# Five rows of one chunk, dealt unevenly over the DMA engines: Pool's software queue over 5 and 11 of them, sync over four

## The chip, the cores and the metric

The kernel runs on one core of a Trainium2 chip. The metric is the device time of one execution in microseconds. A profile's span is shorter than the time by about 1.3 us. "Before" and "changed" are the two kernels; the chunks are counted from 0 in the code, so that "the fourth chunk" is chunk 3.

The profile counts 16 DMA engines. A DMA shows there as packets: a 4 MB chunk as 128 packets of 32 KB. Its semaphore gets sixteen increments, which are read here as the ends of the sixteen engines' shares; in the kernel before, those of chunk 1's load lie between 22.30 and 22.77 us.

## The reference, cut to what matters

```python
x = randn(16, 2048, 256)          # float32: 32768 rows of 1 KB
y = x @ W + scale * (((x @ lora_A) * lora_E) @ lora_B)
```

The kernel folds the low-rank part into one 256x256 matrix (`weff`). What remains is to read 33.55 MB of `x`, multiply, and write 33.55 MB.

## The kernel before

`x` is cut into 8 chunks of 4 MB. In a chunk, partition p holds 32 consecutive rows, so that a chunk's load is one DMA of 128 partitions with 32 KB each. Six chunks have a home in SBUF; the result overwrites the chunk and is stored from there.

```python
x_chunks = x_flat.rearrange("(c p b) k -> c p b k", p=P, b=ROWS)     # P = 128, ROWS = 32
...
ORDER = ["L0", "L1", "L2", "L3", "L4", "L5",
         "S0", "S1", "L6", "L7", "S2", "S3", "S4", "S5", "S6", "S7"]
...
def load(pc):                                   # in sync_program
    c, s, e = pc
    if c == N_HOMES - 1:
        sync.wait_ge(s_weff, 1)
    if c >= N_HOMES:
        sync.wait_ge(stored_of[c - N_HOMES], 16)
    ins = sync.dma_start(out=home(c)[:, s:e, :], in_=x_chunks[c, :, s:e, :])
    return ins.then_inc(loaded[pc], 16)
...
for g in range(N_GROUPS):                       # in gpsimd_program; a group is 4 rows
    ...                                         # waits for the piece of x that starts here
    gpsimd.tensor_copy(out=stage[g % NS][:], in_=home(c)[:, b:b + CG, :]).then_inc(s_stage, 1)
```

Pool casts to bf16, PE transposes, ACT copies, PE multiplies, DVE copies the result back over the chunk.

Of the kernel before, what the change touches and what calls it, by code (L numbers as in the profile page):

```python
# [13 lines left out]
ROWS = 32  # L14
# [9 lines left out]
EARLY_AFTER = 1  # L24

HELD = N_HOMES - 1

CG = 4
GPC = ROWS // CG
# [8 lines left out]
def kernel(  # L38
# [13 lines left out]
    N, K = x_flat.shape  # L52
# [5 lines left out]
    x_chunks = x_flat.rearrange("(c p b) k -> c p b k", p=P, b=ROWS)  # L58
    y_chunks = out_flat.rearrange("(c p b) m -> c p b m", p=P, b=ROWS)

    sbuf, psum, sem = nc.alloc_sbuf_tensor, nc.alloc_psum_tensor, tc.alloc_semaphore
# [21 lines left out]
    loaded = {pc: sem(f"loaded_{pc[0]}_{pc[1]}") for pc in pieces}  # L83
    set_up_loaded = {n: sem(f"loaded_{n}") for n in ("w", "a", "b", "e")}
    stored_of = {c: sem(f"stored_{c}") for c in range(N_CHUNKS - N_HOMES)}
    stored_rest = nc.alloc_semaphore("stored_rest")
    s_ident = sem("ident_made")
    s_pe_set_up = sem("pe_set_up")
    s_ate = sem("ate_made")
# [10 lines left out]
    def home(c):  # L100
        return homes[c % N_HOMES]

    sync, gpsimd, scalar, vector, tensor = nc.sync, nc.gpsimd, nc.scalar, nc.vector, nc.tensor
# [17 lines left out]

    nc.at_finalize(ahead_of_entry_barrier)

    def sync_program():
        def load(pc):
            c, s, e = pc
            if c == N_HOMES - 1:
                sync.wait_ge(s_weff, 1)
            if c >= N_HOMES:
                sync.wait_ge(stored_of[c - N_HOMES], 16)  # L130
            ins = sync.dma_start(out=home(c)[:, s:e, :], in_=x_chunks[c, :, s:e, :])
            return ins.then_inc(loaded[pc], 16)

        opening.append(load(pieces[0]).ins.name)
        for step in ORDER:
            c = int(step[1:])
            if step[0] == "L":
                for pc in pieces:
                    if pc[0] == c and pc != pieces[0]:
                        load(pc)  # L140
                if c == EARLY_AFTER:

                    sync.wait_ge(s_first, 1)
                    sync.dma_start(out=y_chunks[0, :16, 0, :32], in_=home(0)[:16, 0, :32]).then_inc(s_early, 16)
            else:
                sync.wait_ge(s_chunk, c + 1)
                if c == 0:
                    sync.wait_ge(s_early, 16)
                sync.dma_start(out=y_chunks[c], in_=home(c)[:]).then_inc(stored_of.get(c, stored_rest), 16)

    def gpsimd_program():
        gpsimd.memset(ident[:], 0.0).then_inc(s_ident, 1)  # L152
        gpsimd.wait_ge(s_ident, 1)
        gpsimd.affine_select(  # L154
            out=ident[:],
            in_=ident[:],
            compare_op=ALU.not_equal,
            fill=1.0,
            base=0,
            pattern=[[-1, P]],  # L160
            channel_multiplier=1,
        ).then_inc(s_ident, 1)
        for g in range(N_GROUPS):
            c, b = g // GPC, g % GPC * CG
            for pc in pieces:
                if pc[0] == c and pc[1] == b:
                    gpsimd.wait_ge(loaded[pc], 16)
            if (c, b) == (HELD, 0):
                for held_by in stored_of.values():
                    gpsimd.wait_ge(held_by, 16)  # L170
            if g >= NS:
                gpsimd.wait_ge(s_turned, g - NS + 1)
            gpsimd.tensor_copy(out=stage[g % NS][:], in_=home(c)[:, b:b + CG, :]).then_inc(s_stage, 1)  # L173

        gpsimd.wait_ge(s_turned, N_GROUPS - NS + 1)
        gpsimd.drain().then_inc(s_stage, 2)
# [91 lines left out]
    with tc.tile_critical(no_gpsimd_drain=True):  # L268
        sync_program()
        gpsimd_program()  # L270
        scalar_program()
        vector_program()
        tensor_program()
# [35 lines left out]
```

## Time and profile before

| | before |
|---|---|
| time, median (all runs of the first comparison) | 161.78 us (161.56 to 161.97) |
| span of the profiled run | 160.5 us |
| sync's DMA queue, share of 16 engines | 97.9% |
| busiest compute engine | PE, 59% |

From the profile's page of the kernel before. "DMA" is the busy share of the 16 DMA engines in 40 slices of the span, in tenths; "GB/s" is what they moved in each slice. The queue lines give packets, MB, and the share of 16 engines' span. The last lines are of the chain that ended last and of two groups of instructions (busy us, mean ns, idle us before them and what ended it).

```profile
span 160.5 us, 2160 instructions
...
DMA  7999999999999999999999999999999999999993
GB/s 262 432 425 466 449 393 425 490 392 408 498 400 392 492 400 400 400 417 466 425 400 451 457 392 433 474 402 425 466 400 433 466 408 433 449 425 417 441 449 155
...
q1 hardware_dynamic: 2624, 67.11, 97.9%
q10 hardware_dynamic: 352, 0.30, 0.5%
...
HBM read 33.85 MB, written 33.56 MB: 420 GB/s over the span
...
PE 11%; DVE 1%; issue 0%
PE psum_y L236 8%; PE psum_xt L228 4%; DVE home L213 1%
...
L173 POOL CAST stage<-home 128x1024 bf16<-128x1024 f32 x64 | 66.3, 1040 | 47.5 <-PE psum_xt L228 21.4
...
L208 DVE TENSOR_TENSOR weff<-home,psum_y 128x512 bf16<-128x512 f32 x1 | 0.7, 689 | 5.9 <-DMA home<-in_W_dram 5.9
```

The DMA engines are busy in every slice, while the chain of work that ended last covers only 12% of the span: after it, stores drain. `weff` waits for the load of W.

From the view of stretches of the same profile: stretch in us from the span's start, its length, busy us of PE, its weight loads, DVE, ACT and Pool with their instruction counts, then PE's granted clock, the DMA share, and GB/s.

```profile
core 0: us, PE busy (x) PEld busy (x) DVE busy (x) ACT busy (x) POOL busy (x), PEclk, DMA share, GB/s
4.00:24.00 20.00, 14.95 (x86) 11.41 (x87) 8.15 (x8) 8.00 (x8) 9.44 (x10) 1.00 1.03 436
24.00:40.00 16.00, 15.99 (x147) 14.92 (x148) 13.88 (x13) 12.05 (x12) 13.12 (x13) 1.00 0.99 426
40.00:46.00 6.00, 6.00 (x58) 5.58 (x57) 5.66 (x5) 4.51 (x6) 4.65 (x6) 1.00 1.02 437
46.00:58.00 12.00, 12.00 (x113) 11.16 (x111) 11.24 (x10) 9.32 (x10) 9.57 (x10) 1.00 1.02 438
```

The trace also records each DMA packet (start, duration, bytes) and each increment of a DMA's semaphore. A 32 KB packet takes 1.213 us, and the next on its engine starts 3 ns before it ends, hence 27.1 GB/s an engine. The first landings of chunks 1 to 4 are 9.7 us apart (22.30, 32.02, 41.73, 51.45 us), eight such packets: an engine moves 8 of a chunk's 128 partitions. The sixteen increments of the last store are read as the ends of the sixteen engines. This listing is worked out from those records, in us from the span's start:

```
last store, before:   158.45 158.47 158.48 158.70 158.75 158.78 158.80 158.83
                      158.88 158.89 158.90 158.93 159.18 159.44 159.62 160.42
chunk 1 loaded, before: 22.30 to 22.77        chunk 4 loaded, before: 51.45 to 51.92
```

One engine is 0.8 us behind the next. Its 32 KB packets took about 80 ns more than the others', from 100 to 124 us, while stores and compute ran together (two more did from 64 to 66 us). To relieve such an engine is the obvious idea.

### The profile page before, as it was taken

What the parts mean: (1) busy time and instruction counts of PE and PEld (TensorE: products, weight loads), DVE (VectorE), ACT (ScalarE), POOL (GpSimd) and SP (SyncE); (2) the same over time, 40 slices, a digit from 0 to 9 for tenths busy, and PEclk for the clock granted to TensorE, in tenths of its full rate; (3) what the DMA queues carried; (4) which work ended last, traced back from release to release, by engine and by line L of the source; (5) the groups of instructions that cost most, each with busy time, mean ns of one, the idle gap of its engine ahead of it and who ended that gap; (6) DMA issues with size and microseconds to landing.
All of it is one profiled execution on the core that took longest, in us unless ns stands there. A gap on an engine that the chain in (4) does not pass through costs nothing. (4 is left out here: it accounts for less than half of the span.)

```text
span 160.5 us, 2160 instructions
## 1 busy us (share of the span) xinstructions
PE 94.2 (59%) x782; PEld 83.9 (52%) x782; DVE 79.5 (50%) x66; ACT 66.0 (41%) x65; POOL 67.0 (42%) x70
## 2 busy tenths in 40 slices
PE   0585979999999999400019999999990000000000
PEld 0354869999999999300017999899990000000000
DVE  0102796999999999700003799899993000000000
ACT  3240667777777777400005577777740000000000
POOL 1542648777777777000045577777700000000000
PEclk9999999999999999955555999999998555555555
DMA  7999999999999999999999999999999999999993
GB/s 262 432 425 466 449 393 425 490 392 408 498 400 392 492 400 400 400 417 466 425 400 451 457 392 433 474 402 425 466 400 433 466 408 433 449 425 417 441 449 155
DMA packets 2979, 67.43 MB, mean 420 GB/s; under 512 B 528, under 2 KB 544, under 8 KB 672
## 3 DMA queue, kind: packets, MB, share of 16 engines
q1 hardware_dynamic: 2624, 67.11, 97.9%
q10 hardware_dynamic: 352, 0.30, 0.5%
q14 instruction: 3, 0.02, 0.0%
HBM read 33.85 MB, written 33.56 MB: 420 GB/s over the span
## 5 line engine op out<-in xcount | busy, mean ns | idle before, releaser
L213 DVE COPY home<-psum_y 128x1024 f32<-128x1024 f32 x64 | 78.3, 1225 | 30.0 <-PE psum_y L236 25.3
L173 POOL CAST stage<-home 128x1024 bf16<-128x1024 f32 x64 | 66.3, 1040 | 47.5 <-PE psum_xt L228 21.4
L193 ACT COPY xt<-psum_xt 128x1024 bf16<-128x1024 bf16 x64 | 64.7, 1012 | 49.8 <-PE psum_xt L228 49.8
L236 PE MATMUL psum_y<-weff,xt 128*128 128x256 bf16 x512 | 69.4, 281 | 2.6 <-PEq L221 2.5
L236 PEld LDWEIGHTS psum_y<-weff,xt 128*128 128x128 bf16 x512 | 51.4, 101 | 9.6 <-issue 3.2
L228 PE MATMUL psum_xt<-ident,stage 128*128 128x128 f32 x264 | 42.5, 287 | 18.6 <-PEq L221 18.6
L228 PEld LDWEIGHTS psum_xt<-ident,stage 128*128 128x128 f32 x264 | 33.1, 149 | 21.1 <-issue 20.2
L198 DVE TENSOR_SCALAR home<-psum_y,e_sb 16x256 f32<-16x256 f32 x1 | 0.5, 472 | 6.6 <-DMA e_sb<-in_lora_E_dram 6.6
L208 DVE TENSOR_TENSOR weff<-home,psum_y 128x512 bf16<-128x512 f32 x1 | 0.7, 689 | 5.9 <-DMA home<-in_W_dram 5.9
L248 PE MATMUL psum_y<-ident,home 128*16 128x128 f32 x2 | 0.6, 394 | 5.1 <-DMA home<-in_lora_A_dram 5.1
L248 PEld LDWEIGHTS psum_y<-ident,home 128*16 128x16 f32 x2 | 0.1, 87 | 5.1 <-issue 5.1
L193 ACT ACT_TABLE_LOAD x1 | 1.3, 1283 | 2.5 <-issue 2.5
L254 PE MATMUL psum_y<-home 16*128 16x256 f32 x4 | 2.1, 670 | 0.2 <-DMA home<-in_lora_B_dram 0.2
L254 PEld LDWEIGHTS psum_y<-home 16*128 16x128 f32 x4 | 1.2, 319 | 0.8 <-DMA home<-in_lora_B_dram 0.6
L152 POOL MEMSET ident<- 128x128 f32 x1 | 0.2, 204 | 0.7 <-SPq L268 0.7
L154 POOL TENSOR_SCALAR_AFFINE_SELECT ident<-ident 128x128 f32<-128x128 f32 x1 | 0.3, 292 | 0.2 <-POOL ident L152 0.2
L290 POOL MEMSET const-float32-0.0<- 128x1 f32 x1 | 0.1, 98 | 0.2 <-issue 0.2
L290 POOL MEMSET const-bfloat16-1.0<- 128x1 bf16 x1 | 0.1, 101 | 0.0
L290 POOL MEMSET const-uint8-127<- 128x1 uint8 x1 | 0.1, 101 | 0.0
L290 POOL MEMSET const-float32-1.0<- 128x1 f32 x1 | 0.1, 98 | 0.0
## 6 DMA issues: line engine op xcount, KB each, us to landing
out_dram<-home SPq DMA_DIRECT2D x8, 4096.0 KB, 39.7
home<-in_x_dram SPq DMA_DIRECT2D x7, 4096.0 KB, 20.8
home<-in_x_dram SPq DMA_DIRECT2D x2, 1024.0 KB, 5.7
home<-in_x_dram SPq DMA_DIRECT2D x1, 2048.0 KB, 11.5
home<-in_W_dram ACTq DMA_DIRECT2D x1, 256.0 KB, 10.9
home<-in_lora_A_dram ACTq DMA_DIRECT2D x1, 16.0 KB, 4.9
e_sb<-in_lora_E_dram ACTq DMA_DIRECT2D x1, 0.1 KB, 5.5
home<-in_lora_B_dram ACTq DMA_DIRECT2D x1, 16.0 KB, 5.8
```

Source lines behind the costliest of these rows:

```text
L152: gpsimd.memset(ident[:], 0.0).then_inc(s_ident, 1)
L154: gpsimd.affine_select(out=ident[:], in_=ident[:], compare_op=ALU.not_equal, fill=1.0, base=0, pattern=[[-1, P]], channel_multiplier=1,).t ...
L173: gpsimd.tensor_copy(out=stage[g % NS][:], in_=home(c)[:, b:b + CG, :]).then_inc(s_stage, 1)
L193: scalar.copy(out=xt[g % NX][:], in_=halves).then_inc(s_xt, 1)
L198: vector.tensor_scalar(out=ate, in0=psum_y[0][:R, :KT, :P], scalar1=e_sb[:], scalar2=float(scale), op0=ALU.mult, op1=ALU.mult,).then_inc(s ...
L208: vector.tensor_add(out=weff[:], in0=w_sb, in1=psum_y[1][:, :KT, :]).then_inc(s_free, NY)
L213: vector.tensor_copy(out=home(c)[:, b:b + CG, :], in_=psum_y[g % NY][:]).then_inc(s_free, 1)
L228: ins = tensor.transpose(psum_xt[i % NT][:, b, :], words[:, b, :], ident[:])
L236: ins = tensor.matmul(psum_y[i % NY][:, b, :], xt[i % NX][:, b, t, :], weff[:, t, :], start=(t == 0), stop=(t == KT - 1),)
L248: ins = tensor.transpose(psum_y[0][:R, t, :P], a_sb[:, t, :], ident[:])
L254: ins = tensor.matmul(psum_y[1][:, t, :], ate[:, t, :], b_sb, start=True, stop=True)
L290: nc = _bacc.Bacc("TRN2", target_bir_lowering=False, num_devices=1)
```

## The change

The intent is to take some 35 KB off one engine. The last five rows of each partition of chunk 3, 40 KB an engine, leave its load and are dealt anew: by Pool's software queue in the opening, in pieces meant for 5, 11, 5 and 11 engines, and by sync right after chunk 3, in pieces meant for 4 and 2.

```diff
+SPREAD = 3
+TAIL = 5
+SHORT = 2
...
+    def spread_piece(engine, lo, hi, b, e, **kw):
+        engine.dma_start(
+            out=home(SPREAD)[lo:hi, b:e, :], in_=x_chunks[SPREAD, lo:hi, b:e, :], **kw
+        ).then_inc(loaded_tail[engine is gpsimd], 16)
...                                                        # in sync's load()
+            if c == SPREAD:
+                e -= TAIL
             ins = sync.dma_start(out=home(c)[:, s:e, :], in_=x_chunks[c, :, s:e, :])
-            return ins.then_inc(loaded[pc], 16)
+            ins.then_inc(loaded[pc], 16)
+            if c == SPREAD:
+                for lo, hi, b, e in ((0, 68, ROWS - SHORT, ROWS), (66, 68, ROWS - TAIL, ROWS - SHORT)):
+                    spread_piece(sync, lo, hi, b, e)
+            return ins
...                                                        # in gpsimd_program, before the groups
+        mid = ROWS - SHORT
+        for lo, hi, b, e in ((123, 128, ROWS - TAIL, mid), (68, 123, ROWS - TAIL, ROWS), (123, 128, mid, ROWS), (0, 66, ROWS - TAIL, mid)):
+            spread_piece(gpsimd, lo, hi, b, e, max_dma_last_dim=(e - b) * K * 2)
         for g in range(N_GROUPS):
             c, b = g // GPC, g % GPC * CG
+            if c == SPREAD and b < ROWS - TAIL <= b + CG:
+                gpsimd.wait_ge(loaded_tail[0], 16 * 2)
+                gpsimd.wait_ge(loaded_tail[1], 16 * 4)
```

(Two semaphores are allocated besides.)

## The prediction

> **What bounds the kernel now.** The DMA engines. The page's slice line shows DMA at 9 tenths in every slice but the first and last; the queue table gives the sync queue 97.9% of 16 engines' span for 67.11 MB. No compute engine is over 59% busy, and the chain that ended last is over at 122 us of 160.5: after it only six stores drain. The issue timeline has the last store queued at 122 us, so the queues never run dry.

> Every engine gets 8 partitions of every chunk, the same bytes. In the packet records a 32 KB packet takes 1.213 us, the next starts 3 ns before it ends: 128 such per engine are 155 us. So the end is the end of the slowest engine. The 16 increments of the last store's semaphore land at 158.45 to 158.93 us (twelve engines), 159.18, 159.44, 159.62 (these three each carried one 8 KB instruction fetch, 0.31 us) and 160.42. The last engine's packets took about 80 ns more each, between 100 and 124 us, while compute and stores overlap; it alone sets the last 0.8 us.

> **What the change does.** It moves 40 KB per engine (5 rows, 8 partitions) out of the fourth chunk's load and deals them unevenly. [...]Pool's 5+11+5+11 add 5 KB to five engines and 43 KB to eleven. [...]fifteen engines carry 39 to 43 KB instead of 40, and one only 5 KB: minus 35 KB, at 27 GB/s 1.3 us. No run has shown this yet. I take the intent to be that the spared engine is the slow one; the trace does not number engines.

> **Cost.** 43 KB for 40 is 0.11 us; the small packets cost more (2 KB took 84 ns in the W load, against 76 at the 32 KB rate): together an estimated 0.2 us on the other engines. Pool issues four DMAs after 1.9 us; its first cast began at 4.84 us, so I expect it at 6 to 9 us. That is not critical: weff waited for W (landed 12.87 us), and sync had 5 us of queued loads when the first group was done (17 us against 22.3).

> **Sum.** If the slow engine is spared, it ends near 159.2, and the engines with an instruction fetch lead: 159.62 + 0.2 = 159.8, a gain of 0.6 us, so 161.25. If another is spared, the slow engine carries 0.2 more: 162.05. [...]Weights 0.6, 0.25, 0.15: I predict 161.4 us, range 160.9 to 162.4. Faster by over 2%: 0.01; within 2%: 0.97; slower: 0.02.

> **What would show it.** The last store's sixteen landings: the outlier at +0.8 us gone, one engine early or level, the rest 0.2 us later. The fourth chunk's semaphore: one engine through its share 1.3 us early from there on. Pool's first cast later, weff and the issue of the third load hardly. The Pool queue as a new line of about 0.48 MB.

> **What would make it wrong.** Another engine is the slow one in the timed runs; the slow packets are of the profile alone; [...]the Pool DMAs spread over all 16 engines.

In that deal sync's pieces put 34 or 37 KB on four of the five engines with 5 KB, so that with the eleven fifteen engines carry 39 to 43 KB. The sum came to 161.4 us, range 160.9 to 162.4. Of its three cases two are left, 161.25 us (weight 0.6) and 162.05 us (0.25); the third (0.15, 162 to 163.4 us), in which sync's pieces fall on other engines, is cut. The weighted mean of all three, with the third at its middle, would be 161.7.

## The result, and the profile after

| | before | changed |
|---|---|---|
| time, median | 161.78 us | 166.34 us (165.52 to 167.00) |
| span of the profiled run | 160.5 us | 165.1 us |

The ratio is 1.028, with a 95% interval of 1.0232 to 1.0328. Here and below a ratio is the mean time of one kernel's fast runs over that of the other's fast runs of the same rounds, so not quite the ratio of the medians that are quoted.

The same lines of the changed kernel's page, with the new queue (q0, Pool's) and Pool's DMA issues:

```profile
span 165.1 us, 2167 instructions
...
DMA  7999999999999999999999999999999999999993
GB/s 255 376 307 375 302 423 445 405 450 430 365 379 445 445 405 455 405 445 445 413 461 405 447 437 413 437 423 453 421 413 461 413 453 421 437 437 421 445 429 151
...
q1 hardware_dynamic: 2700, 66.60, 96.7%
q0 software_dynamic: 240, 0.51, 1.0%
...
L195 POOL CAST stage<-home 128x1024 bf16<-128x1024 f32 x64 | 66.4, 1040 | 48.2 <-PE psum_xt L250 18.6
...
L230 DVE TENSOR_TENSOR weff<-home,psum_y 128x512 bf16<-128x512 f32 x1 | 0.7, 689 | 9.0 <-DMA home<-in_W_dram 9.0
...
L130 POOL DMA_DIRECT2D home<-in_x_dram x4 | 2.6, 660 | 0.3 <-issue 0.3
```

And of the view of stretches:

```profile
core 0: us, PE busy (x) PEld busy (x) DVE busy (x) ACT busy (x) POOL busy (x), PEclk, DMA share, GB/s
4.00:24.00 20.00, 12.62 (x54) 8.94 (x55) 3.79 (x5) 5.06 (x5) 8.01 (x9) 1.00 1.03 354
24.00:40.00 16.00, 13.11 (x109) 11.65 (x107) 10.85 (x9) 8.91 (x9) 9.05 (x9) 0.89 1.00 428
40.00:46.00 6.00, 6.00 (x58) 5.59 (x56) 5.60 (x5) 4.51 (x6) 4.65 (x6) 1.00 1.07 390
46.00:58.00 12.00, 12.00 (x113) 11.15 (x111) 11.18 (x10) 9.32 (x10) 9.58 (x10) 1.00 0.97 415
```

This is the result in two columns. From 4 to 24 us the DMA share is 1.03, as before, and the rate is 354 GB/s where it was 436: 20 us times 82 GB/s are 1.6 MB, or 3.9 us at 420 GB/s. From 40 to 46 us it is 390 where it was 437. The engines were never idle; they were busy and moved less. A share above 1 is no sign of the loss, since it stands before the change too (1.03): packets' durations overlap, by 3 ns between those of 32 KB. And a packet of one size can take longer: the 16 KB packets took a median of 855 ns here and 616 ns before.

The view counts a packet whole in the stretch in which it starts, so the rates are grainy: one 32 KB packet on each of 16 engines is 0.52 MB, which makes 26 GB/s in a stretch of 20 us and 87 GB/s in one of 6 us. A finer measure from the same packet records spreads the bytes of each packet over its duration, and asks how much later the changed kernel has moved as many bytes as the kernel before. This lag is 3.9 us at 22 us (on the clock of the kernel before) and 4.9 us at 46 us, stays there until 58 us, and ends at 4.4 us. So the loss lies in these two stretches, and the 415 where it was 438 from 46 to 58 us is the shift and the grain.

The issues of Pool's queue in the view of DMAs (size, us from issue to landing):

```profile
home<-in_x_dram POOLq DMA_DIRECT2D x1, 275.0 KB, 11.5
...
home<-in_x_dram POOLq DMA_DIRECT2D x1, 198.0 KB, 19.0
...
home<-in_x_dram POOLq DMA_DIRECT2D x1, 15.0 KB, 7.2
home<-in_x_dram POOLq DMA_DIRECT2D x1, 10.0 KB, 13.0
```

Half a megabyte took until 23 us to land. The rest of the opening did move, as these lines show: W's load made `weff` late (9.0 us of idle time before it instead of 5.9), but this did not matter, since sync still issued its next load at 20.9 us, long before its queue was empty (chunk 1 landed at 26.3 us). The landings, listed from the semaphore records:

```
chunk 1 loaded:  26.26 26.35 26.36 26.38 26.55 | 27.74 27.83 27.83 27.91 27.99 28.03 28.09 28.29 28.32 28.66 | 29.36
chunk 4 loaded:  54.91 | 56.30 56.34 56.37 56.44 56.56 56.63 56.65 56.66 56.70 56.72 56.78 56.92 56.95 57.27 57.98
last store:     162.74 162.90 162.96 162.98 162.99 163.02 163.10 163.16 163.37 163.38 163.39 163.57 163.58 163.70 164.10 165.05
```

Three things can be read from it.

- The deal is as predicted. In chunk 1 five engines (with 5 KB of Pool's) are some 1.5 us ahead of eleven (with 43 KB), from first landing to first landing. In chunk 4 one engine is 1.4 us ahead of all others.
- That engine is the slow one: in the packet records, the engine whose 32 KB packets take about 80 ns more (from 64 to 73 us and from 103 to 128 us) is the one that was ahead in chunk 4. Some 25 such packets, 2 us in all, use up its lead and more: its last data packet ends at 163.12 us, as the twelfth of the sixteen (the first ends at 162.37). It is no longer the last, but it is not the first either.
- But all sixteen are late, also the five with only 5 KB, and also the spared one. Chunk 1's first landing is 3.96 us later than before, and 5 KB are worth 0.2 us of that.

So the step "together an estimated 0.2 us on the other engines" is wrong by 20 times, for engines that carried nothing more as well. The question of the experiments is what makes all engines slow while a small part of the bytes moves.

### The profile page after: what moved, and what is told of

It is laid out like the page before. It is cut to its first block, busy times and chain, and to the rows that moved or that the text cites. A ratio compares the mean times of both kernels' runs of the same rounds, so it can differ in the third digit from the quotient of the medians.

```text
span 165.1 us, 2167 instructions
## 1 busy us (share of the span) xinstructions
PE 95.7 (58%) x782; PEld 84.7 (51%) x782; DVE 79.4 (48%) x66; ACT 66.1 (40%) x65; POOL 69.7 (42%) x74
## 5 line engine op out<-in xcount | busy, mean ns | idle before, releaser
L258 PE MATMUL psum_y<-weff,xt 128*128 128x256 bf16 x512 | 70.2, 283 | 4.8 <-PEq L243 4.6
L250 PE MATMUL psum_xt<-ident,stage 128*128 128x128 f32 x264 | 43.3, 290 | 18.4 <-PEq L243 18.4
L130 POOL DMA_DIRECT2D home<-in_x_dram x4 | 2.6, 660 | 0.3 <-issue 0.3
```

Of the source, the lines that this page charges most:

```text
L130: engine.dma_start(out=home(SPREAD)[lo:hi, b:e, :], in_=x_chunks[SPREAD, lo:hi, b:e, :], **kw).then_inc(loaded_tail[engine is gpsimd], 16)
L250: ins = tensor.transpose(psum_xt[i % NT][:, b, :], words[:, b, :], ident[:])
L258: ins = tensor.matmul(psum_y[i % NY][:, b, :], xt[i % NX][:, b, t, :], weff[:, t, :], start=(t == 0), stop=(t == KT - 1),)
```

## The experiments

The rivals, as they are named in the expectations: (A) whatever moves through Pool's software queue costs all engines; (B) short reads 32 KB apart in HBM cost, whatever the queue; (C) the uneven bytes, or the smaller number of engines; (D) an engine has full speed only into the group of 8 partitions that it fills in a 128-partition DMA, and two engines into one group halve each other; (E) the addresses in HBM, read in another order; (F) a packet outside the engine's own group is slow by itself; (G) software DMAs on fewer than 16 engines. D came up after the first batch. All edits are against the changed kernel, if nothing else is said.

| run | edit in a word | median us | ratio to before (95%) |
|---|---|---|---|
| e1_pool_even | tail by Pool, one DMA of 128 partitions | 162.03 | 1.0021 (1.0001 to 1.0042) |
| e2_act_even | the same by ACT | 161.88 | 1.0012 (0.9993 to 1.0031) |
| e3_sync_fifteen | tail by sync, 120 partitions, then 8 | 163.59 | 1.0109 (1.0092 to 1.0127) |
| e4_pool_tiny | before, with four tiny Pool DMAs | 162.11 | 1.0023 (1.0005 to 1.0040) |
| e5_sync_one | tail by sync, 1 DMA of 128 partitions | 161.89 | 1.0005 (0.9980 to 1.0029) |
| e6_sync_halves | tail by sync, 2 DMAs of 64 | 163.54 | 1.0103 (1.0073 to 1.0134) |
| e7_sync_sixteens | tail by sync, 8 DMAs of 16 | 163.54 | 1.0109 (1.0085 to 1.0133) |
| e8_fifteen_near | e3 with a contiguous source | 163.68 | 1.0110 (1.0086 to 1.0133) |
| e9_sixteens_paired | e7 in another order | 164.94 | 1.0163 (1.0103 to 1.0222) |
| t1_pool_own | Pool, 4 DMAs of 32 partitions | 162.14 | 0.9988 (0.9930 to 1.0045) |
| t2_pool_other | t1 in another order | 166.59 | 1.0269 (1.0206 to 1.0332) |
| t3_pool_halves | Pool, 2 DMAs of 64 | 165.02 | 1.0157 (1.0098 to 1.0215) |
| p1_sync_part | sync's pieces alone | 163.20 | 1.0074 (1.0021 to 1.0127) |
| p2_pool_part | Pool's pieces alone | 166.45 | 1.0249 (1.0190 to 1.0308) |
| p3_change_again | the change, unedited | 165.88 | 1.0235 (1.0184 to 1.0287) |

Before had a median of 161.78 and 161.79 us in the two first batches; 162.65 in the third (e9, t1 to t3), where its runs scattered from 161.66 to 163.25; and 161.70 in the last (p1 to p3), from 161.47 to 162.75. Within those two batches the kernels are better compared with one another. e8, t1 and t2 gave wrong results on purpose; the others were correct.

### First batch: the queue, the addresses, or the deal

e1_pool_even. All five rows by Pool, evenly; sync's pieces gone.

```diff
-        for lo, hi, b, e in ((123, 128, ...), (68, 123, ...), (123, 128, ...), (0, 66, ...)):
-            spread_piece(gpsimd, lo, hi, b, e, max_dma_last_dim=(e - b) * K * 2)
+        spread_piece(gpsimd, 0, P, ROWS - TAIL, ROWS, max_dma_last_dim=TAIL * K * 2)
-                for lo, hi, b, e in ((0, 68, ...), (66, 68, ...)):      # sync's
-                    spread_piece(sync, lo, hi, b, e)
```

> The same five rows early by Pool's queue, but as one DMA of 128 partitions, 40 KB on every engine; no sync pieces. Theory A (anything that Pool's software queue moves in the opening costs all engines throughput): the first whole-chunk load lands 3 to 4 us later than before beyond its share of moved bytes, time 165 to 166.5. Theory B (short reads 32 KB apart in the opening, whatever the queue): the same 165 to 166.5. Theory C (the uneven deal, or the sync pieces at 43 us): loss gone, 161.5 to 162.5.

It measured 162.03 us. More bytes went through Pool's queue than in the changed kernel (0.66 against 0.51 MB), and only some 0.3 us was lost (the interval of the ratio just excludes 1). The row of its opening in the view of stretches:

```profile
4.00:24.00 20.00, 14.93 (x86) 11.36 (x86) 7.18 (x7) 7.67 (x8) 8.25 (x8) 1.00 1.02 418
```

418 GB/s is within the grain of the 436 of the kernel before.

e2_act_even. The same DMA, issued by ACT to its hardware queue.

```diff
+        spread_piece(scalar, 0, P, ROWS - TAIL, ROWS)       # after the loads of A, E, B and W
```

> The same one DMA of five rows of 128 partitions, in the opening, but issued by ACT to its hardware queue after W. Theory A: no loss, 161.5 to 162.3. Theory B: as slow as by Pool, 165 to 166.5. This and the run by Pool tell A from B.

It measured 161.88 us. A and B both fall: with an even deal neither queue costs more than some 0.3 us.

e3_sync_fifteen. No Pool DMA; the tail by sync, after chunk 3.

```diff
-                for lo, hi, b, e in ((0, 68, ...), (66, 68, ...)):
-                    spread_piece(sync, lo, hi, b, e)
+                spread_piece(sync, 0, 120, ROWS - TAIL, ROWS)
+                spread_piece(sync, 120, P, ROWS - TAIL, ROWS)
```

> No Pool DMA: the five rows by sync right after the fourth chunk[...]. If the engine that the changed kernel spares is the last of the sixteen, and that is the slow one, the outlier in the last store's landings goes and the time is 161.0 to 161.5. If the slow engine is another, 161.9 to 162.3 (5 KB more on it or none). If short reads 32 KB apart cost all engines about 1 us wherever they stand: 162 to 163.

It measured 163.59 us, outside all three ranges. The slow engine was not spared (the outlier in the last store's landings stayed: 162.70 after 161.55), but that alone would be 162. The row from 40 to 46 us, in which the tail is loaded:

```profile
40.00:46.00 6.00, 6.00 (x57) 5.57 (x56) 5.71 (x5) 4.81 (x5) 4.90 (x5) 1.00 1.03 282
```

The packet records say how. A tail packet of 5 KB takes 196 ns in e1 and e2 (median). In e3 the median is 364 ns, with 10% at 415 or more. And the one engine that had no tail piece (so fifteen had), and so was the first to start a packet of chunk 4, took 2368 ns for it instead of 1213. Its packet belongs to a load of 128 partitions like all others, so other engines' tail packets must have slowed it. On the other fifteen too the first packet of chunk 4 took 1.5 to 2.5 us, part of it perhaps waiting behind their own tail packets.

e4_pool_tiny. The kernel before, with Pool DMAs of 5, 55, 5 and 66 partitions, as in the change, but of 512 B a partition, into a scratch tile.

```diff
+        for lo, hi, n in ((123, 128, 0), (68, 123, 0), (123, 128, 1), (0, 66, 0)):
+            gpsimd.dma_start(
+                out=probe[lo:hi, n:n + 1, :], in_=x_chunks[3, lo:hi, ROWS - 1:, :PROBE], max_dma_last_dim=PROBE * 2
+            ).then_inc(s_probe, 16)
```

> The kernel before with four Pool DMAs of the same 5, 55, 5, 66 partitions but 512 B a partition into a scratch tile (67 KB in all, nothing else changed; output unaffected). Theory A in the form of a fixed price for each software DMA or for the queue being in use: 2 to 4 us slower. A in the form of a price per byte or per packet sharing an engine: under 1 us slower. B: under 0.7 us.

It measured 162.11 us, 0.3 us over before, so there is no large fixed price of four such DMAs.

### Second batch: the same rows by sync, in pieces of other sizes

e5_sync_one, e6_sync_halves and e7_sync_sixteens load the tail by sync after chunk 3 in one, two or eight DMAs. In each of them, as planned, all 16 engines carry the same 40 KB; for two and eight DMAs this is not shown here.

```diff
+            if c == SPREAD:
+                for lo in range(0, P, n):           # n = 128, 64, 16
+                    spread_piece(sync, lo, lo + n, ROWS - TAIL, ROWS)
```

> Control: the five tail rows by sync right after the fourth chunk, as one DMA of 128 partitions. All theories: packets of 5 KB take 196 ns as in the even runs, no loss, 161.6 to 162.1.

> The same rows as two DMAs of 64 partitions[...]. Theory D (each engine has full speed only into its own group of 8 partitions, and two engines into one group halve each other): 5 KB packets near 390 ns, the tail phase 3.0 instead of 1.5 us, time 163.0 to 163.6. Theory C (only uneven bytes or fewer engines cost): no loss, 161.6 to 162.1.

> The same rows as eight DMAs of 16 partitions[...]. Theory D: [...]packets up to 780 ns, the phase up to 6 us, time 164 to 166.5. Theory C: no loss beyond 7 more DMA ends (some 10 ns each per engine), 161.6 to 162.3.

They measured 161.89, 163.54 and 163.54 us. If the deal was as planned, uneven bytes (C) are not needed for the loss. The row from 40 to 46 us, for one, two and eight DMAs in turn:

```profile
40.00:46.00 6.00, 6.00 (x57) 5.58 (x56) 5.63 (x5) 4.81 (x5) 4.93 (x5) 1.00 1.04 442
```

```profile
40.00:46.00 6.00, 6.00 (x58) 5.59 (x56) 5.63 (x6) 4.81 (x5) 4.93 (x5) 1.00 1.06 326
```

```profile
40.00:46.00 6.00, 6.00 (x58) 5.57 (x56) 5.71 (x5) 4.77 (x5) 4.85 (x5) 1.00 1.03 300
```

The share is 1.03 to 1.06 in all three, the rate 442, 326 and 300 GB/s. The median 5 KB packet took 196, 348 and 381 ns. The lag behind the kernel before grows by 0.1, 1.8 and 1.9 us from 40 to 46 us. The expectation for eight DMAs was wrong in size (packets up to 780 ns, 164 to 166.5 us): it counted four engines to a group, the measured median, 381 ns, is near that of two (2 x 196 ns). Neither count is shown by itself. If pieces that follow each other (0-15, 16-31, ...) fall into different groups, their order should matter: that was a hint for a sharper test (e9). (The 10 ns of a DMA's end in theory C are measured: the 4-byte packets, sixteen for each of sync's 19 DMAs in the kernel before, took 9 ns each.)

e8_fifteen_near. As e3, but each tail is read from rows that lie side by side in HBM.

```diff
+                rows = x_flat[SPREAD * ROWS * P:SPREAD * ROWS * P + P * TAIL, :].rearrange("(p b) k -> p b k", b=TAIL)
+                for lo, hi in ((0, 120), (120, P)):
+                    sync.dma_start(out=home(SPREAD)[lo:hi, ROWS - TAIL:, :], in_=rows[lo:hi]).then_inc(...)
```

> [...]the same destinations, but the source rows lie side by side in HBM instead of 32 KB apart; the result is wrong on purpose. Theory D (the destination decides): 5 KB packets again near 390 ns, 163.3 to 163.9. Theory E (the addresses in HBM, read in another order by 15 engines, decide): back to near 196 ns and 161.9 to 162.2.

It measured 163.68 us, with a median packet of 367 ns. The row:

```profile
40.00:46.00 6.00, 6.00 (x58) 5.56 (x56) 5.71 (x5) 4.62 (x5) 4.71 (x5) 1.00 1.05 281
```

281 GB/s against e3's 282: the source's addresses do not matter, so E falls.

### Third batch: only the order of the pieces changes

e9_sixteens_paired. e7 with the eight pieces reordered: 0-15 is followed by 32-47, then 16-31 by 48-63, and so on. By D, two in a row then meet in the same groups.

```diff
-                for lo in range(0, P, 16):
+                for lo in (0, 32, 16, 48, 64, 96, 80, 112):
```

> As the run with eight sync DMAs of 16 partitions, only their order changed[...]. Theory D (a group takes one engine's rate in all): [...]5 KB packets near 780 ns, the tail phase up to 6 us, time 164.5 to 166.5. Theory F (a packet outside an engine's own group runs at half rate by itself, whoever shares): 390 ns and 163.5 as before.

It measured 164.94 us, the median packet took 542 ns and the longest 724. The row:

```profile
40.00:46.00 6.00, 6.00 (x58) 5.58 (x56) 5.66 (x5) 4.51 (x6) 4.66 (x6) 1.00 1.05 192
```

192 GB/s against 300 for the same pieces in order, and a lag that grows by 3.5 us instead of 1.9 (e7 ran in another batch; these numbers of the traces carry the comparison). A packet outside the own group that is slow by itself (F) would have stayed at 381 ns. What counts is which pieces are under way together. The time lies in the range that D gave; the median packet, at 542 ns, lies between the 390 ns of two engines to a group and the 780 ns of four, so four were perhaps reached only in part.

t1_pool_own and t2_pool_other. Pool in the opening, four DMAs of 32 partitions. Only the order of the pieces differs: by it, as supposed, an engine writes its own group in t1 and another's in t2. (The source is shaped 8x4 with a gap, by which the author meant each DMA to use 8 engines; the traces do not show the number. The rows are thus wrong, in both runs alike.)

```diff
+        for lo in (0, 64, 32, 96):          # t1; t2: (64, 0, 96, 32)
+            near = min(lo, P - 40)
+            gpsimd.dma_start(
+                out=home(SPREAD)[lo:lo + 32, ROWS - TAIL:, :],
+                in_=x_chunks[SPREAD, near:near + 40, ROWS - TAIL:, :].rearrange("(a b) r k -> a b (r k)", b=5)[:, :4],
+            ).then_inc(loaded_tail[1], 16)
```

> Pool's queue in the opening again, the five rows in four DMAs of 32 partitions[...], in the order 0-31, 64-95, 32-63, 96-127[...]. Theory D: no loss, 161.9 to 162.3 like the one even Pool DMA. Theory G (software DMAs on fewer than 16 engines cost by themselves): 163.5 to 166.

> The same four Pool DMAs in the order 64-95, 0-31, 96-127, 32-63[...]. Wrong on purpose as before. Theory D: 5 KB packets near 390 ns and a loss in the opening of the order of the changed kernel's, 163.5 to 166. Theory G: the same as the run in the other order.[...]

They measured 162.14 and 166.59 us, on the same chip in the same rounds. They differ in the order alone: G, which gave both the same time, falls. t1 lost nothing clear of this batch's scatter. t2 lost more than D's range (up to 166), and its Pool packets took less than the 390 ns that D gave, so D was right on which order costs and wrong on the sizes. The openings, t1 first:

```profile
4.00:24.00 20.00, 15.30 (x86) 11.71 (x86) 7.31 (x8) 7.89 (x8) 8.75 (x9) 1.00 1.04 437
```

```profile
4.00:24.00 20.00, 12.38 (x52) 8.65 (x53) 3.61 (x4) 5.06 (x5) 7.69 (x8) 1.00 1.04 351
```

437 and 351 GB/s, with equal bytes, queue and packets (0.66 MB in 320 packets of Pool's queue in both). This is the changed kernel's opening (354) made and unmade by the order of four pieces. In t2 it is less Pool's packets that are long (median 230 ns against 196) than sync's: its 16 KB packets took 809 ns against 611. In the changed kernel they took 855 against 616 before. The order may also change which engine reads which rows of the source. That this is the cause is unlikely: in t1 the source rows are shifted against the partitions and no loss is seen, and in e8 another source changed nothing.

t3_pool_halves. Pool in the opening, two DMAs of 64 partitions, a correct result.

```diff
+        for lo in (0, 64):
+            spread_piece(gpsimd, lo, lo + 64, ROWS - TAIL, ROWS, max_dma_last_dim=TAIL * K * 2)
```

> Pool's queue in the opening, five rows in two DMAs of 64 partitions[...], correct result. Theory D: [...]loss of 1.5 to 3 us, 163.3 to 165. Theory C or G (uneven or fewer engines): no loss, 161.9 to 162.3.

It measured 165.02 us. The row of its opening:

```profile
4.00:24.00 20.00, 11.82 (x49) 8.19 (x50) 3.61 (x4) 4.68 (x5) 6.67 (x7) 1.00 1.04 356
```

That is 2.9 us slower than t1 in the same rounds and 3.0 us slower than the one even DMA of e1 (on another chip). The author planned all 16 engines with equal bytes, which is not shown here; if it was so, the uneven bytes (C) and the number of engines (G) are not needed for the loss in the opening either. t1 and t2, 4.45 us apart with equal pieces, need no such plan.

### Last batch: the two parts of the change, each alone

p1_sync_part loads the tail early and evenly as e1 does, then lets sync load its two pieces over it again. p2_pool_part keeps Pool's four pieces, then lets sync load all 32 rows of chunk 3.

```diff
+            if c == SPREAD:                                   # p1, in sync's load()
+                sync.wait_ge(loaded_tail[1], 16)
+                for lo, hi, b, e in ((0, 68, ...), (66, 68, ...)):
+                    spread_piece(sync, lo, hi, b, e)
-            if c == SPREAD:                                   # p2, in sync's load()
-                e -= TAIL
+            if c == SPREAD:
+                sync.wait_ge(loaded_tail[1], 16 * 4)
```

> Sync's part alone: the tail comes early as one even Pool DMA (162.03 in its own run), and sync then loads its two pieces (68 partitions over 4 engines, 2 over 2) over it once more, the same values, 0.14 MB more. Theory D: [...]about 1 us over the even run for all engines, plus 0.3 us of bytes, 163.0 to 164.0.[...]

> Pool's part alone: its four pieces in the opening, then the whole fourth chunk by sync in one 128-partition DMA (0.51 MB twice, the same values). The extra bytes are worth 1.2 us. Theory D: 3 us of loss and 1.2 us of bytes, 165.5 to 166.8. If the pieces cost only their bytes, 163.0 to 163.4.

> The changed kernel itself, unedited, beside the two parts on one chip: 165.5 to 167.0, as before; its loss should be that of Pool's part without the extra bytes (3 us) plus that of sync's (1 us), less than 1 us unexplained.

They measured 163.20, 166.45 and 165.88 us, with 161.70 before. The rows in which each part works, p1 from 40 to 46 us and p2 from 4 to 24 us:

```profile
40.00:46.00 6.00, 6.00 (x58) 5.58 (x57) 5.66 (x5) 4.51 (x6) 4.58 (x6) 1.00 0.97 342
```

```profile
4.00:24.00 20.00, 13.70 (x66) 9.99 (x67) 5.04 (x6) 6.07 (x6) 9.01 (x10) 1.00 1.04 354
```

Had p1's 34 KB on four engines delayed these alone, they would have landed chunk 4 some 1.3 us later (34 KB at 27.1 GB/s) and the other twelve not; D expected all to be late. All were. Chunk 4 landed from 52.70 to 54.43 us, in e1 from 51.96 to 52.84: even the earliest is 0.7 us later, though twelve engines had no share in the pieces (by the six increments that the same two pieces have in the changed kernel's records). The sum, in medians over before: p1 1.5 us, less 0.3 for e1's own loss and 0.3 for bytes loaded twice, is 0.9. p2 is 4.75 us, less 1.2 for its bytes, 3.5. Together they make 4.4 us, the change 4.2 us. By means, with this batch's scatter of before, it is 0.6 plus 3.0 against 3.8. Pool's part is thus about four fifths of the loss, sync's about one fifth, and no third cause of more than some 0.3 us is needed.

## Why the prediction was wrong, point by point

The prediction was 161.4 us, between 160.9 and 162.4; the kernel measured 166.34 us.

- **What bounds the kernel** (the engines, never without queued work): right, and still so after the change. The share stayed at 1 (9 tenths in every slice of the page but the first and last).
- **How the pieces are dealt, and that the spared engine is the slow one:** right. Five, eleven and one engine are told apart in the landings, and the engine with the 80 ns longer packets is the one that was ahead. That it would be this engine was taken from the change's intent, at a weight of 0.6, and not from the trace.
- **"W and the first group have slack":** right. `weff` came 3.5 us later (16.42 instead of 12.95 us), more than the "hardly" of the prediction, and cost nothing.
- **Pool's first cast "at 6 to 9 us":** wrong and harmless. It began at 4.95 us instead of 4.84; each of the four issues held Pool for 0.66 us.
- **"Together an estimated 0.2 us on the other engines":** this step failed. The engines were costed one by one, by the bytes and packets of their own shares, as if an engine's rate did not depend on what the others move. The measured cost was 4 us on every engine (chunk 1's first landing 3.96 us later). What is measured in its place: pieces of fewer than 128 partitions can slow the loads beside them, and the order alone makes or unmakes it (t1 and t2, 4.45 us apart). What would explain it is D: such pieces send engines into the groups of others, which those are filling at that very time, and both wait. No trace shows the groups.
- **"Another engine is the slow one; the slow packets are of the profile alone; 16 engines":** three of the four named risks; the fourth: that Pool's issues hold it for over 10 us. Pool's issues took 2.6 us in all and the landings fell into 5 and 11, so neither this one nor the 16 engines occurred; the profiled runs take the same time as the others, so nothing speaks for the one of the profile alone, and the first was not seen. The risk that did occur, pieces that slow each other, was not on the list, and a loss over 2% was given a chance of 0.02.
- **The outlier in the last store "gone":** the old one was, but one of the eleven was behind instead (165.05 against 164.10 us). It fell behind already in the opening. Why that one did is open.

The gain itself was also thought of wrongly. If the group of partitions is the limit as well as the engine, then its bytes take their time whichever engine brings them. The spared engine had 35 KB less and still landed chunk 4 at 54.91 us, where the kernel before had all of it by 51.92. By D it was ahead of the others only because they had lost more. This last conclusion is argued from D and from these landings; no run dealt the bytes unevenly with every packet in its own group. No version that beats the kernel before was found here.

Open is the size of the loss: in t2 an engine carries on average 40 KB of Pool's packets (foreign ones, by D), 1.5 us of transfer at 27.1 GB/s, and the kernel loses 4.45 us. If each foreign packet takes twice its time and also delays the group's own engine as long, that makes an estimated 8 x 2 x 0.196 = 3.1 us, and Pool's packets did not take twice their time (230 ns against 196). The packet records of t2 and t1 show where the loss sits: per engine, t2's packets took 0.3 us more on Pool's queue, 0.2 us more in the load of W, and 3.9 us more in sync's own loads (0.1 on the 8 KB packets, 1.6 on the 16 KB, 2.1 on the first ten of 32 KB), 4.4 us together. Pool's small packets cost sync's large ones far more than themselves; why so much more than their own 1.5 us is open. Also open is why one engine's packets are longer (by 80 ns) when stores and compute overlap.

## What to carry to other kernels

In a kernel like this one, whose DMA engines are full, keep every DMA at 128 partitions, and cut along the rows, not along the partitions: here one DMA of 5 rows by 128 partitions cost 0.1 to 0.3 us on each of three queues, while two of 64 partitions cost 1.7 to 3 us. When you cost a transfer, ask not only how many bytes each engine gets but also what it does to the transfers beside it: the same four pieces cost nothing clear of the scatter in one order and 4.45 us more in another (t1, t2); that it is a matter of who else writes to the same partitions is theory D, not shown. And read the DMA share beside the GB/s: a share of 1 with a fallen rate meant longer packets here (1.03 at 354 GB/s instead of 436), and the packet durations, matched against those of the same size elsewhere, show which.
